# Sums of Strassen products formed in PSUM banks across products, in a hybrid encoder layer

## The chip, the cores and the metric

The kernel runs on one core of one Trainium2 chip. The core has a matrix engine (TensorE, PE in the views, with its weight loads as PEld), three engines for elementwise work (VectorE or DVE, ScalarE or ACT, GpSimd or POOL) and SyncE (SP), which here issues most DMA transfers. Each engine works through its own instructions in program order and waits on semaphores for the others. Matmuls write to PSUM, eight banks of 512 fp32 values on each of 128 partitions; everything else lives in SBUF. The metric is the device time of one execution in microseconds (us), as the median of several runs.

## The reference

One layer, fp32, 1024 tokens of width 1024:

```python
h = rmsnorm(x, norm_mix[l])
proj = h @ w_in[l]
q, k, v, r, lr_f, lr_b, u, g_a, g_b = jnp.split(proj, split_points, axis=-1)
...
o = o_fwd + o_bwd                              # gated linear attention, both directions
...
y_a = o @ w_branch_gla[l]
...
merged = jax.nn.sigmoid(g_a) * y_a + jax.nn.sigmoid(g_b) * y_b
x = x + merged @ w_out[l]
h2 = rmsnorm(x, norm_ffn[l])
gate, up = jnp.split(h2 @ w_ffn_in[l], 2, axis=-1)
x = x + (jax.nn.silu(gate) * up) @ w_ffn_out[l]
return rmsnorm(x, norm_final)
```

The hidden width of the feed-forward part (D_FF) is 2816, so w_ffn_in is 1024 x 5632. The change touches the last four products: w_branch_gla, w_out, w_ffn_in and w_ffn_out.

## The kernel before

**Three matmuls for one.** For fp32 accuracy each operand is split in a high and a low part (split_to, L172 and L173: a ScalarE cast makes the high part, named dh, gh, wh or oh, and VectorE or GpSimd subtracts it to get the low part, dl, gl, wl or ol). A product is then high x high, high x low and low x high, three matmuls (products, at L250) added up in one PSUM bank, with a contraction of 128 each.

**Strassen's seven products.** Each of the four large matrix products is cut in 2 x 2 quarters and done as the seven products of the Strassen-Winograd form, numbered P1 to P7, in place of eight. The four result quarters are

```
C00 = P1 + P2        C01 = P1 + P6 + P5 + P3
C10 = P1 + P6 + P7 + P4        C11 = P1 + P6 + P7 + P5
```

Operand sums go in ahead (VectorE and GpSimd); sums of products are formed after. Before, each product is added up in its own PSUM bank or banks, taken in turn from a cycle over all eight (mm_banks, three banks of the pool ps_mm, then five of ps_g). The collector reads it from there, and VectorE and GpSimd add the products in SBUF.

**The stages.** From 0 to about 575 us run the input projection, attention and pooling, which the change leaves alone. Then:

- Branch projection (BRANCH, o @ w_branch_gla) and merged projection (MERGED, merged @ w_out), by the function project: 48 matmuls a product, in four banks (m = 0..3) with c = 0 and 1 for the two halves of the contraction. After c = 1 each m is collected. collect_branch adds the products up in u2 and v2, and merge (L1041 to L1043) multiplies by the gate and adds the pooled branch, the latter on GpSimd. collect_out adds to the rows x2 of the residual, squares them for the norm (squares, L1224) and normalises them (xn).
- FFN-in: the normalised rows are transposed (L1176, L1179) and their quarter sums formed (features, L1194 to L1214), with their splits gh and gl, which stay for the whole stage. The weights come in 22 units of 128 gate channels and the 128 up channels that belong to them; one unit's seven products have 12 matmuls each in one bank. Gated.run collects them. The first three units run interleaved, product by product, while the features are still being made (units 0 and 1 through all seven products, unit 2 through P1 and P2); units 2 to 21 then run one by one, with the weight sums (combined, L1101, tile fs) and splits of coming products some four steps ahead (AHEAD). After each odd unit put_out (L1361 to L1364) forms the four operand sums for FFN-out on VectorE and sends seven pieces to DRAM; OutSums forms the weight sums for FFN-out on GpSimd (L1380 to L1386).
- FFN-out: 132 matmuls a product in four banks, the contraction in pieces that come back from DRAM (gor, wor) and are split into oh and ol. collect (L1549 and plus, L1510) adds each product into the residual rows x2; whole, second_half and first_half normalise and store the result.

**What sets the order.** The program's order is written out by hand: tuples of product numbers (BRANCH, MERGED, ORDER for FFN-in, OUT_ORDER) and explicit steps between them. Each engine keeps that order, so an instruction whose input is late holds up all that stand behind it on its engine.

## Time and profile before

| | |
|---|---|
| median of 3 runs | 1451.91 us (1451.48 to 1453.66) |
| profiled execution | 1452.8 us, of which the span of the trace is 1451.1 us |
| mean granted TensorE clock | 0.995 |
| instructions in the trace | 18652, of them 6797 matmuls |
| HBM read / written | 158.22 MB / 74.71 MB |

The views give times from the span's start, in us. A row of a timeline has start, duration, engine, line, operation and tiles (out<-in); in brackets stands how long the engine had been idle before it, and what it was released by. A row with x2 or more joins instructions that follow one another. A row of the chain has start, duration and the work that set the end there. The idle time of an engine that others don't wait for costs nothing.

### The profile page before, as it was taken

To read this page: it belongs to the slowest core of one execution; us is meant where nothing else is said; L and a number is where in the kernel's file an instruction comes from. 1 tells how busy PE (TensorE), PEld (TensorE's weight loads), DVE (VectorE), ACT (ScalarE), POOL (GpSimd) and SP (SyncE) were. 2 spreads that over 40 slices of the span, in tenths; PEclk is the share of its full clock that TensorE was granted. 3 is DMA by queue.
4 is the path that set the end of the run, shared out by engine and by line. 5 is a ranking of instruction groups with operands and counts; after the bars stand their busy time and mean duration, and the time that the engine had idled before them with its cause. 6 is when DMAs were issued, how large, how long until landed. Compare 5 with 4: busy or idle time off the path is not lost. (4 is left out here: it accounts for less than half of the span.)

```text
span 1451.1 us, 18652 instructions
## 1 busy us (share of the span) xinstructions
PE 1405.5 (97%) x6797; PEld 1179.6 (81%) x6797; DVE 872.5 (60%) x1111; ACT 561.8 (39%) x995; POOL 743.8 (51%) x510
## 2 busy tenths in 40 slices
PE   7999999999999999999999989999999999999988
PEld 6889898888888787888777778888888888778876
DVE  6266767662132463477994777777677777465375
ACT  6364655652122333344125523322323323444243
POOL 3240413222264553456743457666666668597355
PEclk9999999999999999999999999999999999999999
DMA  6120201011176768686666556444544446966362
GB/s 186 44 58 2 59 16 44 15 30 37 50 224 206 274 214 293 236 290 252 191 203 225 182 178 195 152 154 160 163 153 152 151 154 222 351 234 255 131 240 79
DMA packets 164732, 234.15 MB, mean 161 GB/s; under 512 B 10873, under 2 KB 97953, under 8 KB 164641
## 3 DMA queue, kind: packets, MB, share of 16 engines
q1 hardware_dynamic: 151936, 194.17, 40.7%
q10 hardware_dynamic: 12704, 38.80, 7.1%
q8 instruction: 53, 0.87, 0.2%
q14 instruction: 39, 0.31, 0.1%
HBM read 158.22 MB, written 74.71 MB: 161 GB/s over the span
## 5 line engine op out<-in xcount | busy, mean ns | idle before, releaser
L173 POOL TENSOR_TENSOR wl<-raw,wh 128x512 fp32r<-128x512 f32 (+1 forms) x91 | 124.6, 1387 | 257.3 <-ACT wh L172 212.4
L250 PE MATMUL ps<-gh,wl 128*128 128x512 f32 x616 | 240.8, 391 | 4.0 <-POOL wl L173 4.0
L250 PE MATMUL ps<-gh,wh 128*128 128x512 f32 x616 | 240.9, 391 | 0.1
L250 PE MATMUL ps<-gl,wh 128*128 128x512 f32 x616 | 240.2, 390 | 0.0
L250 PE MATMUL ps<-hh,wh 128*128 128x512 f32 x576 | 229.3, 398 | 5.2 <-ACT wh L172 5.2
L250 PE MATMUL ps<-hh,wl 128*128 128x512 f32 x576 | 226.1, 393 | 1.2 <-POOL wl L173 1.2
L250 PE MATMUL ps<-hl,wh 128*128 128x512 f32 x576 | 225.4, 391 | 0.0
L173 POOL TENSOR_TENSOR wl<-fs,wh 128x512 fp32r<-128x512 f32 x80 | 112.4, 1405 | 97.9 <-ACT wh L172 69.7
L250 PEld LDWEIGHTS ps<-gh,wl 128*128 128x128 f32 x616 | 116.0, 188 | 29.2 <-POOL wl L173 4.8
L172 ACT CAST wh<-fs 128x512 fp32r<-128x512 f32 x80 | 49.8, 622 | 230.2 <-DVE fs L1101 221.4
L250 PEld LDWEIGHTS ps<-gh,wh 128*128 128x128 f32 x616 | 116.1, 189 | 24.3 <-issue 0.5
L250 PEld LDWEIGHTS ps<-gl,wh 128*128 128x128 f32 x616 | 115.9, 188 | 23.8
L173 POOL TENSOR_TENSOR ol<-gor,oh 128x1024 fp32r<-128x1024 f32 (+1 forms) x42 | 109.2, 2617 | 47.0 <-ACT oh L172 46.1
L250 PEld LDWEIGHTS ps<-hh,wh 128*128 128x128 f32 x576 | 108.9, 189 | 27.0 <-ACT wh L172 6.0
L250 PEld LDWEIGHTS ps<-hh,wl 128*128 128x128 f32 x576 | 108.9, 189 | 25.3 <-POOL wl L173 2.1
L250 PEld LDWEIGHTS ps<-hl,wh 128*128 128x128 f32 x576 | 109.1, 189 | 21.3
L250 PE MATMUL ps<-oh,ol 128*128 128x512 f32 x308 | 120.2, 390 | 4.9 <-POOL ol L173 4.9
L250 PE MATMUL ps<-ol,oh 128*128 128x512 f32 x308 | 120.0, 389 | 2.9 <-DVE ol L173 2.9
L250 PE MATMUL ps<-oh,oh 128*128 128x512 f32 x308 | 120.0, 390 | 0.0
L173 DVE TENSOR_TENSOR ol<-wor,oh 128x1024 fp32r<-128x1024 f32 (+1 forms) x42 | 87.6, 2112 | 39.0 <-ACT oh L172 30.2
L173 POOL TENSOR_TENSOR wl<-fraw,wh 128x512 fp32r<-128x512 f32 x60 | 94.3, 1571 | 16.3 <-ACT wh L172 16.3
L250 PE MATMUL ps<-wh,hh 128*128 128x256 f32 x256 | 79.7, 311 | 0.0
(255 smaller groups left out, 2878.3 us busy)
## 6 DMA issues: line engine op xcount, KB each, us to landing
raw<-in_w_in_dram SPq DMA_DIRECT2D x88, 256.0 KB, 3.1
fraw<-in_w_ffn_in_dram SPq DMA_DIRECT2D x44, 512.0 KB, 5.6
gor<-g_out SPq DMA_DIRECT2D x35, 512.0 KB, 5.4
g_out<-s SPq DMA_DIRECT2D x44, 256.0 KB, 2.4
wor<-t_out SPq DMA_DIRECT2D x20, 512.0 KB, 8.2
g_out<-g SPq DMA_DIRECT2D x33, 256.0 KB, 3.4
x<-in_x_dram SPq DMA_DIRECT2D x16, 512.0 KB, 4.6
wor<-in_w_ffn_out_dram SPq DMA_DIRECT2D x15, 512.0 KB, 7.4
```

The source lines that it names most:

```text
L172: nc.scalar.copy(hi, src)
L173: eng.tensor_tensor(lo, src, as_f32(hi), op=ALU.subtract)
L250: nc.tensor.matmul(ps, a[i], b[j], start=first and n == 0, stop=last and n == 2)
```

## The change

Products that share their sums now go on in the same PSUM banks. P1, P6, P7 and P4 form one group: only P1 starts its bank afresh, and each later one is added on top (start is false), so that the bank holds P1, then P1 + P6, then P1 + P6 + P7, then C10 without more. P5 and P3 form a second group; P2 takes banks of the second kind by itself. A group of four-bank products uses U_BANKS (three of ps_mm, one of ps_g) or X_BANKS (four of ps_g), and a unit of FFN-in has one bank of ps_mm and one of ps_g. The collector reads the partial sum between two products of a group: by a ScalarE copy for P1, P6 and P5 in the branch projection and FFN-in, by VectorE additions elsewhere. In the merged projection the groups are P1, P6, P7, P2, P3 (with P2 and P3 starting afresh) on U_BANKS, and P4 and P5 on X_BANKS.

The product orders change with it:

| | before | after |
|---|---|---|
| BRANCH | 1 2 6 5 3 7 4 | 1 2 6 5 7 3 4 |
| MERGED | 1 7 6 5 4 2 3 | 1 4 6 7 5 2 3 |
| ORDER (FFN-in) | 1 6 2 7 4 5 3 | 1 2 6 5 7 3 4 |
| OUT_ORDER (FFN-out) | 1 6 2 5 3 7 4 | 1 2 6 5 3 7 4 |

The buffers p1s and u3 for sums in SBUF go. The diff, cut to its core (the tuples of the orders, the loads that follow them and the buffers for sums are left out):

```diff
     mm_banks = cycle([ps_mm])
-    def products(ps, a, b, first=True, last=True):
+    def products(ps, a, b, first=True, last=True, onto=False):
         for n, (i, j) in enumerate(((0, 0), (0, 1), (1, 0))):
-            nc.tensor.matmul(ps, a[i], b[j], start=first and n == 0, stop=last and n == 2)
-    def mm3(ps, a, b, first, last):
-        products(ps, a, b, first, last)
+            nc.tensor.matmul(ps, a[i], b[j], start=first and n == 0, stop=last and n == 2, skip_group_check=onto)
+    def mm3(ps, a, b, first, last, onto=False):
+        products(ps, a, b, first, last, onto)
         pump(ps.shape[-1] / HALF)
...
+    UP = (1, 6, 7, 4)
+    FIRST = (1, 2, 5)
     add = partial(nc.vector.tensor_tensor, op=ALU.add)
...
                 return merged[i, j][c][:, :, :]
-            if p == 7:
+            if p == 6:
                 s3s.append(slot(s="s3"))
                 sub(s3s[c][:, :, :], block(0, 0), block(1, 0))
-            elif p == 6:
                 padd(block(1, 0), block(1, 0), block(1, 1))
...
     mm_banks = cycle([ps_mm] * MM_BANKS + [ps_g] * (8 - MM_BANKS))
-    def project(base, products, collect, before, amid=None):
+    U_BANKS = [ps_mm] * 3 + [ps_g]
+    X_BANKS = [ps_g] * 4
+    def project(base, products, collect, before, amid=None, first=FIRST, up=UP, pools_of=lambda p: U_BANKS if p == 1 else X_BANKS):
+        banks = {}
         for at, p in enumerate(products):
             before(p)
-            sums = [bank(next(mm_banks)) for _ in range(4)]
+            if p in first:
+                banks[p in up] = [bank(pool) for pool in pools_of(p)]
+            sums = banks[p in up]
             for c in range(2):
...
                             sums[m][:, :], tuple(t[:, m * P : (m + 1) * P] for t in a[k]), b[k],
-                            c == 0 and k == 0, c == 1 and k == 1,
+                            c == 0 and k == 0 and p in first, c == 1 and k == 1, p not in first,
                         )
...
         sa, yb = (quarter(t, m) for t in gates[i, j])
-        add(dst, ps, s)
-        nc.vector.tensor_tensor(dst, dst, sa, op=ALU.mult)
+        if s is not None:
+            add(dst, ps, s)
+            ps = dst
+        nc.vector.tensor_tensor(dst, ps, sa, op=ALU.mult)
         padd(dst, dst, yb)
...
         u, v = quarter(u2, m), quarter(v2, m)
-        if p == 1:
-            nc.scalar.copy(u, ps)
-        elif p == 2:
-            merge(0, 0, m, ps, u)
-        elif p == 6:
-            add(u, ps, u)
-        elif p == 5:
-            add(v, ps, u)
-        elif p == 3:
-            merge(0, 1, m, ps, v)
-        elif p == 7:
-            merge(1, 1, m, ps, v)
-            add(u, ps, u)
+        if p in (1, 6, 5):
+            nc.scalar.copy(v if p == 5 else u, ps)
         else:
-            merge(1, 0, m, ps, u)
+            i, j = {2: (0, 0), 7: (1, 1), 3: (0, 1), 4: (1, 0)}[p]
+            merge(i, j, m, ps, {2: u, 7: v, 3: u}.get(p))
...
     def collect_out(p, m, ps):
-        p1, w = quarter(p1s, m), quarter(u3, m)
-        def x_of(i, j):
-            return x2[4 * (1 - i) + m][:, COLS[j]]
-        if p == 1:
-            nc.scalar.copy(p1, ps)
-            add(x_of(0, 0), x_of(0, 0), p1)
-        elif p == 7:
-            add(w, ps, p1)
-        elif p == 6:
-            add(w, ps, w)
-            add(p1, ps, p1)
-            padd(x_of(1, 1), x_of(1, 1), w)
-        elif p == 5:
-            for i in (1, 0):
-                add(x_of(i, 1), ps, x_of(i, 1))
-            add(x_of(1, 0), x_of(1, 0), w)
-            padd(x_of(0, 1), x_of(0, 1), p1)
-        else:
-            i, j = {4: (1, 0), 2: (0, 0), 3: (0, 1)}[p]
-            add(x_of(i, j), ps, x_of(i, j))
+        for i, j in {1: ((0, 0),), 6: ((0, 1),), 7: ((1, 0), (1, 1)), 5: ((0, 1), (1, 1)), 4: ((1, 0),), 2: ((0, 0),), 3: ((0, 1),)}[p]:
+            xs = x2[4 * (1 - i) + m][:, COLS[j]]
+            add(xs, ps, xs)
+        if p in (5, 2, 3):
             t = 4 * (1 - i) + m
...
                 xn[t] = slot(shape=(D,), s="xn")
-            for col in {4: (0, 1), 2: (0,), 3: (1,)}[p]:
+            for col in {5: (0, 1), 2: (0,), 3: (1,)}[p]:
                 squares(t, mss[t], xn[t], col)
...
             units[0].step(2)
-    project(len(BRANCH) * 2, MERGED, collect_out, before_out, amid_out)
+    project(
+        len(BRANCH) * 2, MERGED, collect_out, before_out, amid_out, (1, 2, 3, 4, 5), (1, 2, 3, 6, 7),
+        lambda p: X_BANKS if p in (4, 5) else U_BANKS
+    )
     normed()
     flush()
-    def product(unit, p, ps):
+    def product(unit, p, ps, right):
         for k in range(4):
             mm3(
-                ps[:, :], unit(p, k), tuple(t[:, k % 2, :] for t in split_b[p][k // 2]),
-                k == 0, k == 3,
+                ps[:, :], unit(p, k), tuple(t[:, k % 2, :] for t in right[p][k // 2]),
+                k == 0 and p in FIRST, k == 3, p not in FIRST,
             )
...
         def __init__(self, unit, in_slot=False):
-            self.unit, self.banks = unit, {}
+            self.unit, self.done = unit, set()
             self.g = slot(s="g") if in_slot else None
...
                 sums = slot(s="sums")
-                self.p16, self.p167 = sums[:, 0, :], sums[:, 1, :]
+                self.gate, self.up = sums[:, 0, :], sums[:, 1, :]
             elif not in_slot:
...
         def two_sums(self):
-            self.p16, self.p167 = t2(s="p16")[:, :], t2(s="p167")[:, :]
+            self.gate, self.up = t2(s="gate")[:, :], t2(s="up")[:, :]
         def run(self, p):
-            self.banks[p] = bank(next(mm_banks))
-            product(self.unit, p, self.banks[p])
-            ps = self.banks[p][:, :]
+            if p == 1:
+                self.u = bank(ps_mm)
+            elif p in FIRST:
+                self.x = bank(ps_g)
+            ps = self.u if p in UP else self.x
+            product(self.unit, p, ps, split_b)
+            self.done.add(p)
+            ps = ps[:, :]
             mul = partial(nc.vector.tensor_tensor, op=ALU.mult)
-            if p > 2:
-                p16, p167 = self.p16, self.p167
             if p == 1:
-                self.p1 = self.g[:, 0, :] if self.g else t2(s="p1")[:, :]
-                nc.scalar.copy(self.p1, ps)
+                self.sg = self.g[:, 0, :] if self.g else t2(s="sg")[:, :]
+                nc.scalar.copy(self.sg, ps)
             elif p == 2:
-                self.sg = self.p1 if 6 in self.banks else self.g[:, 1, :]
-                add(self.sg, ps, self.p1)
+                add(self.sg, ps, self.sg)
                 nc.scalar.activation(self.sg, self.sg, AF.Silu)
             elif p == 6:
-                add(p16, ps, self.p1)
+                nc.scalar.copy(self.gate, ps)
+            elif p == 5:
+                nc.scalar.copy(self.up, ps)
             elif p == 7:
-                add(p167, ps, p16)
-            elif p == 4:
+                add(self.up, ps, self.up)
+            elif p == 3:
+                add(self.gate, ps, self.gate)
+                nc.scalar.activation(self.gate, self.gate, AF.Silu)
+            else:
                 self.g = self.g or slot(s="g")
-                add(self.g[:, 0, :], ps, p167)
-                mul(self.g[:, 0, :], self.g[:, 0, :], self.sg)
-            elif p == 3:
-                add(p16, ps, p16)
-                nc.scalar.activation(p16, p16, AF.Silu)
-                mul(self.g[:, 1, :], p16, p167)
-            if p in (4, 5) and {4, 5} <= self.banks.keys():
-                self.fifth()
-        def fifth(self):
-            for s in (self.p167, self.p16):
-                nc.vector.tensor_tensor(s, self.banks[5][:, :], s, op=ALU.add)
+                mul(self.g[:, 0, :], ps, self.sg)
+            if p in (3, 7) and {3, 7} <= self.done:
+                self.g = self.g or slot(s="g")
+                mul(self.g[:, 1, :], self.gate, self.up)
     def put_out(q, ga, gb):
...
     def collect(p, m, ps):
-        p1 = p1s[m // 2][:, m % 2, :]
-        if p == 1:
-            nc.scalar.copy(p1, ps)
-            plus(nc.gpsimd, 0, 0, m, p1)
-        elif p == 6:
-            nc.vector.tensor_tensor(p1, ps, p1, op=ALU.add)
-            plus(nc.vector, 0, 1, m, p1)
-            for j in (1, 0):
-                plus(nc.gpsimd, 1, j, m, p1)
-        else:
-            for half, j in {2: ((0, 0),), 5: ((0, 1), (1, 1)), 3: ((0, 1),), 7: ((1, 1), (1, 0)), 4: ((1, 0),)}[p]:
-                plus(nc.vector, half, j, m, ps)
+        half, j = {1: (0, 0), 2: (0, 0), 6: (0, 1), 5: (1, 1), 7: (1, 1), 3: (0, 1), 4: (1, 0)}[p]
+        xs = x2[4 * half + m][:, COLS[j]]
+        add(xs, ps, xs)
         if p == 3:
...
+    banks = {}
     for at, p in enumerate(OUT_ORDER):
         closing = at == len(OUT_ORDER) - 1
-        sums = [bank(next(mm_banks)) for _ in range(4)]
+        if p in FIRST:
+            banks[p in UP] = [bank(pool) for pool in (U_BANKS if p == 1 else X_BANKS)]
+        sums = banks[p in UP]
         for i in range(CLOSE if closing else n_of):
```

How instructions move, at three places. A name with a number is one tile; the numbers of the two kernels differ.

On ScalarE, at the start of FFN-in, before: the silu of P2 (L1337) and the casts of the features (gh), then those of weights (wh).

```order
L1337 ACTIVATE g_7196<-g_7196 128x512
L172 CAST gh_7405<-hb_6995 128x1024
L172 CAST gh_7407<-hb_6996 128x1024
L172 CAST gh_7428<-hb_7242 128x1024
L172 CAST gh_7430<-hb_7243 128x1024
L172 CAST wh_7522<-fs_7520 128x512
```

And now, with copies of P5 (L1328) and of P6 (L1326) of units 0 and 1:

```order
L1324 ACTIVATE g_7144<-g_7144 128x512
L172 CAST gh_7353<-hb_6943 128x1024
L172 CAST gh_7355<-hb_6944 128x1024
L1328 COPY sums_7141<-ps_7346 128x512
L172 CAST gh_7377<-hb_7190 128x1024
L172 CAST gh_7379<-hb_7191 128x1024
L1328 COPY sums_7143<-ps_7370 128x512
L1326 COPY sums_7141<-ps_7149 128x512
L1326 COPY sums_7143<-ps_7167 128x512
L172 CAST wh_7468<-fs_7466 128x512
```

The copies came in behind the casts; the matmuls of P7 write to the banks that the L1326 copies read.

On VectorE, at the border between an odd and an even unit of the FFN-in loop, before: P3's and P5's additions, put_out's sums, then the next unit.

```order
L1355 TENSOR_TENSOR p_1555_8058<-ps_8168,p_1555_8058 128x512
L1101 TENSOR_TENSOR fs_8187<-fraw_7964,fraw_7966 128x512
L1347 TENSOR_TENSOR p_1555_8058<-ps_8193,p_1555_8058 128x512
L1349 TENSOR_TENSOR g_8161<-p_1555_8058,p_1556_8059 128x512
L1361 TENSOR_TENSOR s_1588_8209<-g_8009,g_8161 128x512
L1362 TENSOR_TENSOR s_1588_8209<-s_1588_8209,g_8009 128x512
L1363 TENSOR_TENSOR s_1589_8210<-g_8009 128x512
L1364 TENSOR_TENSOR s_1589_8210<-g_8161,s_1588_8209 128x512
L1339 TENSOR_TENSOR p_1590_8222<-ps_8247,p_1595_8241 128x512
L1101 TENSOR_TENSOR fs_8262<-fraw_7964,fs_8142 128x512
```

And now:

```order
L1332 TENSOR_TENSOR gate_7974<-ps_8043,gate_7974 128x512
L1339 TENSOR_TENSOR g_8096<-gate_7974,up_7975 128x512
L1336 TENSOR_TENSOR g_8096<-ps_7982,sg_7995 128x512
L1345 TENSOR_TENSOR s_1535_8119<-g_7951,g_8096 128x512
L1346 TENSOR_TENSOR s_1535_8119<-s_1535_8119,g_7951 128x512
L1347 TENSOR_TENSOR s_1536_8120<-g_7951 128x512
L1348 TENSOR_TENSOR s_1536_8120<-g_8096,s_1535_8119 128x512
L1103 TENSOR_TENSOR fs_8134<-fraw_7887,fraw_7889 128x512
L1103 TENSOR_TENSOR fs_8155<-fraw_7887,fs_8076 128x512
```

The sums now follow P4's multiplication (L1336), and both weight sums (fs) of coming products stand behind them, where one stood ahead.

On VectorE, at the border of the branch and the merged projection, before: the fourth tile of P7, the two splits for the first merged product, its operand sum (L918), and P4's first tile.

```order
L1041 TENSOR_TENSOR mg_6313<-ps_6254,sum_5769 128x512
L1042 TENSOR_TENSOR mg_6313<-mg_6313,gate_6050 128x512
L1059 TENSOR_TENSOR sum_5767<-ps_6254,sum_5767 128x512
L173 TENSOR_TENSOR dl_6369<-mg_5924,dh_6368 128x1024
L173 TENSOR_TENSOR dl_6405<-mg_5925,dh_6404 128x1024
L918 TENSOR_TENSOR s_1210_6408<-mg_5924,mg_6211 128x1024
L1041 TENSOR_TENSOR mg_6416<-ps_6356,sum_5766 128x512
L1042 TENSOR_TENSOR mg_6416<-mg_6416,gate_6140 128x512
```

And now, with P3 in the place of P7:

```order
L1052 TENSOR_TENSOR mg_6301<-ps_6055,sum_5767 128x512
L1054 TENSOR_TENSOR mg_6301<-mg_6301,gate_6046 128x512
L173 TENSOR_TENSOR dl_6349<-mg_5924,dh_6348 128x1024
L173 TENSOR_TENSOR dl_6385<-mg_5925,dh_6384 128x1024
L1054 TENSOR_TENSOR mg_6394<-ps_5778,gate_6136 128x512
L1054 TENSOR_TENSOR mg_6394<-ps_5779,gate_6136 128x512
```

The third operation of each tile has gone, the operand sum stands later, and P4 has one operation a tile.

More of the change, by code (lines that the diff above doesn't have):

```diff
@@ L852, in data_split @@
         return [(hi[:, k, :], lo[:, k, :]) for k in range(2)]
-    BRANCH = (1, 2, 6, 5, 3, 7, 4)
+    BRANCH = (1, 2, 6, 5, 7, 3, 4)
     WEIGHT_A = {1: (0, 0), 2: (0, 1), 4: (1, 1)}
@@ L891 @@
     line += [branch_piece(p, c) for p in BRANCH for c in range(2)]
-    MERGED = (1, 7, 6, 5, 4, 2, 3)
+    MERGED = (1, 4, 6, 7, 5, 2, 3)
     merged = {}
@@ L1046, in collect_branch @@
         u, v = quarter(u2, m), quarter(v2, m)
-        if p == 1:
-            nc.scalar.copy(u, ps)
-        elif p == 2:
-            merge(0, 0, m, ps, u)
-        elif p == 6:
-            add(u, ps, u)
-        elif p == 5:
-            add(v, ps, u)
-        elif p == 3:
-            merge(0, 1, m, ps, v)
-        elif p == 7:
-            merge(1, 1, m, ps, v)
-            add(u, ps, u)
-        else:
-            merge(1, 0, m, ps, u)
+        if p in (1, 6, 5):
+            nc.scalar.copy(v if p == 5 else u, ps)
+        else:
+            i, j = {2: (0, 0), 7: (1, 1), 3: (0, 1), 4: (1, 0)}[p]
+            merge(i, j, m, ps, {2: u, 7: v, 3: u}.get(p))
     x2 = [None] * NT
     def before_branch(p):
-        if p in (1, 6, 5, 3):
-            load_gates(*{1: (0, 0), 6: (0, 1), 5: (1, 1), 3: (1, 0)}[p])
-        if p in (7, 4):
-            for t in range(4 * (p == 7), 4 * (p == 7) + 4):
+        if p in (1, 6, 5, 7):
+            load_gates(*{1: (0, 0), 6: (1, 1), 5: (0, 1), 7: (1, 0)}[p])
+        if p in (3, 4):
+            for t in range(4 * (p == 3), 4 * (p == 3) + 4):
                 x2[t] = slot(shape=(D,), s="x2")
@@ L1073 @@
     project(0, BRANCH, collect_branch, before_branch)
-    ORDER = (1, 6, 2, 7, 4, 5, 3)
+    ORDER = (1, 2, 6, 5, 7, 3, 4)
     xn = [None] * NT
@@ L1232, in two_scale @@
         return rs
-    p1s, u3 = ([slot(s="sum") for _ in range(2)] for _ in range(2))
     mss = {}
@@ L1333, in run @@
             elif p == 2:
-                self.sg = self.p1 if 6 in self.banks else self.g[:, 1, :]
-                add(self.sg, ps, self.p1)
+                add(self.sg, ps, self.sg)
                 nc.scalar.activation(self.sg, self.sg, AF.Silu)
             elif p == 6:
-                add(p16, ps, self.p1)
+                nc.scalar.copy(self.gate, ps)
+            elif p == 5:
+                nc.scalar.copy(self.up, ps)
             elif p == 7:
-                add(p167, ps, p16)
-            elif p == 4:
-                self.g = self.g or slot(s="g")
-                add(self.g[:, 0, :], ps, p167)
-                mul(self.g[:, 0, :], self.g[:, 0, :], self.sg)
-            elif p == 3:
-                add(p16, ps, p16)
-                nc.scalar.activation(p16, p16, AF.Silu)
-                mul(self.g[:, 1, :], p16, p167)
@@ L1389, in sums @@
                 nc.sync.dma_start(t_out[p][:, self.q, :], src)
-    OUT_ORDER = (1, 6, 2, 5, 3, 7, 4)
+    OUT_ORDER = (1, 2, 6, 5, 3, 7, 4)
     PIECES = [(q, min(2, PAIRS - q)) for q in range(0, PAIRS, 2)]
@@ L1494 @@
     x2 = []
-    p1s = [slot(s="p1s") for _ in range(2)]
     gain_final = slot(shape=(D,), s="gfin")
@@ L1506 @@
     scales = {}
-    def plus(eng, half, j, m, src):
-        xs = x2[4 * half + m][:, COLS[j]]
-        eng.tensor_tensor(xs, xs, src, op=ALU.add)
     def whole(t):
@@ L1561, in collect, with piece_product @@
             first_half(4 + m)
-    def piece_product(ps, n, m, first, last):
+    def piece_product(ps, n, m, first, last, onto):
         w, g = ready_pieces[n]
@@ L1568, in piece_product @@
                 ps[:, :], tuple(t[:, q, m * P : (m + 1) * P] for t in g), tuple(t[:, q, :] for t in w),
-                first and q == 0, last and q == c - 1,
+                first and q == 0, last and q == c - 1, onto,
             )
@@ L1585 @@
             for m in range(4):
-                piece_product(sums[m], n, m, i == 0, i == n_of - 1)
+                piece_product(sums[m], n, m, i == 0 and p in FIRST, i == n_of - 1, p not in FIRST)
                 if i == n_of - 1:
@@ L1597 @@
                 for i in range(CLOSE, n_of):
-                    piece_product(sums[m], at * n_of + i, m, False, i == n_of - 1)
+                    piece_product(sums[m], at * n_of + i, m, False, i == n_of - 1, p not in FIRST)
                 collect(p, m, sums[m][:, :])
```

## The prediction

> **What bounds the kernel now.** I read the page's busy times first, then the busy time by stretch, then the chain that ended last, and then the timeline of each engine around the places where TensorE stood idle.

> The page's busy times:

> ```profile
> PE 1405.5 (97%) x6797; PEld 1179.6 (81%) x6797; DVE 872.5 (60%) x1111; ACT 561.8 (39%) x995; POOL 743.8 (51%) x510
> ```

> The busy time of the FFN-in loop, of TensorE, its weight loads, VectorE, ScalarE and GpSimd in this order:

> ```profile
> 862.00:1223.00 361.00, 360.65 (x1585) 298.49 (x1586) 254.29 (x279) 108.58 (x188) 258.45 (x177) 1.00 0.50 166
> ```

> The reader should see that TensorE is the bound, and that in the FFN-in loop it idles 0.35 us of 361. The change keeps all 6797 matmuls. Vector additions that vanish there are therefore worth nothing by themselves: VectorE is busy 254 of those 361 us and has room anyway. Time can only be won from the idle of TensorE outside the loop, and lost wherever a new wait stops it. The chain says the same, one unbroken piece of matmuls:

> ```profile
> 862.35 360.35 PE ps L250 x1582
> ```

> This gives the scale: 360.35 / 1582 = 0.228 us a matmul, 2.73 us for a 12-matmul product of a FFN-in unit, 10.9 us for a 48-matmul product of the projections.

> The idle pieces that the change can touch, from TensorE's timeline, each with what released it:

> ```profile
> 711.70 0.50 PE L250 MATMUL ps<-wh,dl 128*128 128x512 f32 x1 [1.54 <-DVE dl L173]
> 734.64 0.50 PE L250 MATMUL ps<-wh,dl 128*128 128x512 f32 x1 [0.84 <-DVE dl L173]
> ...
> 862.35 0.80 PE L250 MATMUL ps<-gh,wl 128*128 128x512 f32 x1 [3.79 <-POOL wl L173]
> ...
> 865.50 0.40 PE L250 MATMUL ps<-gh,wh 128*128 128x512 f32 x1
> ...
> 1249.50 0.50 PE L250 MATMUL ps<-oh,ol 128*128 128x512 f32 x1 [1.70 <-POOL ol L173]
> ...
> 1306.24 0.50 PE L250 MATMUL ps<-oh,ol 128*128 128x512 f32 x1 [2.01 <-POOL ol L173]
> ...
> 1399.05 0.50 PE L250 MATMUL ps<-ol,oh 128*128 128x512 f32 x1 [2.94 <-DVE ol L173]
> ```

> Together 12.8 us, and the 3.79 us idle costs more than itself: eight starts from 862.35 to 865.50 take 3.15 us where seven steps of 0.228 would take 1.59, so about 1.6 us go to matmuls at half rate (0.80 us the first shown, 0.40 the last).

> **What the change adds.** A product that goes on in a bank may not begin before the collector has read the previous product from it. Before, a product took the next bank in a rotation over eight. Now P6 waits for the copy of P1, P7 for the copy of P6, P4 for the addition of P7, and P3 for the copy of P5. Mostly one whole product lies between, and the copy is short:

> ```profile
> 866.41 0.59 ACT L1332 COPY p<-ps 128x512 f32<-128x512 f32 x1 [4.69 <-PE ps L250]
> ```

> With 2.73 us or more of slack for 0.59 us this costs nothing, unless the copy stands behind something late on its in-order engine. [...] I looked for late readers at each stage.

> **Branch to merged projection, about +1.3 us.** The first merged product reuses the bank group in which the branch's P4 has just ended, so it needs P4's first multiplication, which VectorE runs after two subtractions for the split (dl). VectorE before:

> ```profile
> 700.61 0.68 DVE L1041 TENSOR_TENSOR mg<-ps,sum 128x512 f32<-128x512 f32 x1
> ...
> 709.12 0.68 DVE L1059 TENSOR_TENSOR sum<-ps,sum 128x512 f32<-128x512 f32 x1
> 709.73 3.05 DVE L173 TENSOR_TENSOR dl<-mg,dh 128x1024 fp32r<-128x1024 f32 x2
> ```

> Four tiles of three operations took 9.1 us up to 709.73. Without the third operation (4 x 0.6) they could end at 707.3 to 709.7, the later end if GpSimd's additions hold the multiplications up as here. Then two dl (3.05), then the multiplication (0.68): 711.1 to 713.5, where TensorE started at 711.70 before. I take 713.0, nearer the late end, since the same GpSimd additions remain: +1.3, bounds 0 and +1.8.

> **Merged projection, about -0.1 us.** The third product's operand sums no longer come late, so the 0.84 at 734.64 goes. But each tile of the fifth product now takes two additions from PSUM ahead of its norm in place of one, 0.6 us more a tile by the spacing above; only the last tile's share can reach TensorE, since it works on while the others come. I place that at 0.7. Bounds -0.84 and +1.

> **Start of FFN-in, about +3.5 us.** Three units run interleaved, and unit 0's P7 must wait for the copy of its P6. On ScalarE this copy now stands behind the last casts of the features and two copies of P5. The same casts before, and the GpSimd work that makes VectorE late ahead of them:

> ```profile
> 825.84 1.05 ACT L172 CAST gh<-hb 128x1024 fp32r<-128x1024 f32 x1 [1.72 <-DVE hb L1214]
> 830.33 2.95 ACT L172 CAST gh<-hb 128x1024 fp32r<-128x1024 f32 x3 [3.44 <-DVE hb L1214]
> ```

> ```profile
> 815.53 12.54 POOL L173 TENSOR_TENSOR gl<-hb,gh 128x1024 fp32r<-128x1024 f32 x4 [12.60 <-ACT gh L172]
> ```

> ```profile
> 725.41 2.04 ACT L1253 COPY sum<-ps 128x512 f32<-128x512 f32 x4
> ```

> Nothing ahead of 830.33 gets earlier: VectorE's same order of feature subtractions releases it. So the copy of P6 ends at 830.33 + 2.95 for three casts + 3 x 0.51 = 834.8. Counting products of 12 matmuls from TensorE's timeline, P7 would start with this row:

> ```profile
> 827.50 0.39 PE L250 MATMUL ps<-gh,wl 128*128 128x512 f32 x1
> ```

> That is an idle of 7.3 us. It will cost half-rate matmuls too (1.6 by the rows above). What pays some back is the 3.79 us idle at 862.35, which waits for FFN-out weights that in turn wait for the first outputs. Between 827.5 and 862.35 TensorE has 34.85 - 3.79 = 31.1 us of work, so unit 3 starts at 834.8 + 31.1 + 1.6 = 867.5 at full rate, against 862.35 + 1.6 lost behind it: +3.5. The outputs come some 5 us later, so those weights land about then as well. Bounds: if the copies were not late, -3.8 - 1.6 at best; if the weights wait longer than TensorE, +7.3.

> **FFN-in loop, about +1.4 us.** After nine pairs of units VectorE forms four sums for FFN-out (put_out). These now stand directly ahead of the weight sum whose cast stands on ScalarE ahead of the next unit's copy of P1, and P6 waits for that copy. Undisturbed sums and those in the loop:

> ```profile
> 850.20 0.69 DVE L1361 TENSOR_TENSOR s<-g,g 128x512 f32<-128x512 f32 x1
> ...
> 852.74 0.68 DVE L1101 TENSOR_TENSOR fs<-fraw,fs 128x512 f32<-128x512 f32 x1
> ...
> 922.92 1.67 DVE L1361 TENSOR_TENSOR s<-g,g 128x512 f32<-128x512 f32 x1
> ...
> 928.64 0.68 DVE L1339 TENSOR_TENSOR p<-ps,p 128x512 f32<-128x512 f32 x1
> ```

> From the eviction of P4: multiplication 0.72, sums 2.54, weight sum 0.68, cast 0.63 with its start, copy 0.59 = 5.2 us, against two products, 5.46, less some 0.2 to 0.3 until P4's eviction starts. That is no stall to 0.4 each. With the loop's slow sums (5.72) it is 3.2 us more, nine times 3.2 = 29 us. They were slow because GpSimd was running a weight subtraction:

> ```profile
> 924.71 1.75 POOL L173 TENSOR_TENSOR wl<-fs,wh 128x512 fp32r<-128x512 f32 x1 [0.66 <-ACT wh L172]
> ```

> In the new order the next weight sum, and with it GpSimd's next subtraction, stands behind the sums, so GpSimd has run dry by the second of them. I take the undisturbed row and 0.15 each: +1.4, bounds 0 and 29.

> **End of FFN-in and FFN-out, about -3.3 us.** The last product is now P4 with one multiplication, not P3 with an addition, an activation and a multiplication. VectorE before:

> ```profile
> 1226.98 0.68 DVE L1347 TENSOR_TENSOR p<-ps,p 128x512 f32<-128x512 f32 x1
> 1228.36 0.69 DVE L1349 TENSOR_TENSOR g<-p,p 128x512 f32<-128x512 f32 x1 [0.70 <-ACT p L1348]
> ```

> The last multiplication could run at 1226.98 in place of 1228.36: the last outputs come 1.4 us sooner, off the 1.70 at 1249.50. I take -1.3, bounds 0 and -1.7. GpSimd's twelve additions into x vanish, and with them the 2.01 idle at 1306.24, which these held up:

> ```profile
> 1298.67 5.22 POOL L1510 TENSOR_TENSOR x<-x,p1s 128x512 f32<-128x512 f32 x3
> ```

> -2.0, bounds 0 and -2.0. P3 follows P5 in its banks, and P4 follows P7, but with three tiles between one tile's end and its next start; I put no cost on it. The 2.94 at 1399 hangs on the final norm and stays.

> **Clock.** A new idle near 2.8 us at the start of the merged projection could bring half-rate matmuls. The rows differ: 2.94 us at 1399.05 is followed by a matmul of 0.50 like every short idle, while these two pauses, 3.4 us in all, were followed by matmuls of 0.61:

> ```profile
> 498.69 0.50 PE L250 MATMUL ps<-hh,wh 128*128 128x512 f32 x1 [2.75 <-ACT wh L172]
> ...
> 500.04 0.61 PE L250 MATMUL ps<-hh,wl 128*128 128x512 f32 x1 [0.62 <-POOL wl L173]
> ```

> I leave it out of the sum; with it the sum would be 1.6 higher. [...]

> **Sum.** 1.3 - 0.1 + 3.5 + 1.4 - 3.3 = +2.8 on the profiled execution, 1452.8 around a span of 1451.1 us (1.7 us outside it, unchanged). That execution is 0.9 above the median of the runs, 1451.91, so the forecast is about 1454.7. A measurement here can tell about 0.2%, 2.9 us, from no change: faster is below 1449.0, slower above 1454.8.

> **Rivals.**
> 1. *The new waits are hidden* (0.27). The copies at the start of FFN-in run before P7 needs them and everything else pays: -0.8, -1.3, -2.0 and 2 to 4 of the idle at 862.35, some -7: 1445. For it: ScalarE idles 3.44 us just ahead of 830.33, and another order of release would let copies through. Against it: the engine works in order, and the cast that it waits for stands ahead of the copies.
> 2. *The sums in the loop stay slow* (0.14). Nine stalls of about 3 us, a sum of +2.8 - 1.4 + 29: about 1482; with half of it, 1468. For it: all the loop's sums before are stretched. Against it: the row at 850.20 with GpSimd idle. It decides as soon as the sums take more than 2.9 us.
> 3. *FFN-out stalls on its consecutive products* (0.07). P3's first matmul waits for a late addition of P5, since VectorE also splits the operands there, 1.5 us for each (3.05 for two, above). Two or three of these ahead of each of two product borders, 6 to 9 us over the forecast if nothing lies between: about 1462. Against it: about 4 us (18 matmuls) lie between.

> **How the numbers follow.** The forecast's own case holds 0.52, with a range of 1449 to 1460 from the bounds of its terms. The range for 8 in 10 takes in rival 1 to 1445 and rival 2 with half its stalls: 1445 to 1468. Faster: rival 1 and a little of the forecast, 0.29. Within 0.2%: not quite half of the forecast's case, 0.24. Slower: the other half, rivals 2 and 3, 0.47.

> **What would show it.** In the timeline of TensorE: an idle of about 7 us near 828, released by a ScalarE copy of L1326, then matmuls at half rate; little or no idle near 867; 2 to 3.5 us at 713; none at 735 and 1306. In the loop: the copies of L1321 ending within 5.5 us of P4's multiplication, and put_out's sums taking 2.5 us. I am wrong if the copies at 828 run ahead of the casts, if TensorE shows nine idles of 2 us or more in the loop, or if the weights of unit 3 keep it waiting beyond 868.

## The result, and the profile after

The changed kernel took 1459.33 us (median of 6 runs, 1457.99 to 1462.07) against 1452.33 (6 runs) for the kernel before: slower, ratio 1.005, interval 1.0037 to 1.0063. The forecast was 1454.7, slower was the likeliest case at 0.47, and the range ended at 1468. So direction and mechanism came out as forecast, and the size was 7.0 us where 2.8 had been summed up. The sum alone stood just under the prediction's own line for slower (1454.8); what made the result clear is in good part half clock, which the sum left out.

The page's busy times after the change:

```profile
PE 1408.5 (97%) x6797; PEld 1183.0 (81%) x6797; DVE 724.2 (50%) x995; ACT 583.8 (40%) x1039; POOL 682.1 (47%) x490
```

VectorE is busy 148 us less than before and GpSimd 62 us less, and the span grew from 1451.1 to 1457.8. TensorE was the bound, so the relief bought nothing where TensorE was busy. What changed is where TensorE idles. Its timeline, with the idle ahead of each row and what ended it:

```profile
712.88 0.76 PE L251 MATMUL ps<-wh,dh 128*128 128x512 f32 x1 [2.92 <-issue]
713.44 0.63 PE L251 MATMUL ps<-wl,dh 128*128 128x512 f32 x1
...
804.89 0.33 PE L1178 MATMUL tr<-ident,xn 128*128 128x128 f32 x1 [1.27 <-DVE xn L287]
...
837.91 0.80 PE L251 MATMUL ps<-gh,wh 128*128 128x512 f32 x1 [7.54 <-ACT sums L1326]
...
871.69 0.50 PE L251 MATMUL ps<-gh,wl 128*128 128x512 f32 x1 [1.36 <-POOL wl L173]
...
1257.89 0.50 PE L251 MATMUL ps<-oh,ol 128*128 128x512 f32 x1 [1.42 <-POOL ol L173]
...
1405.09 0.79 PE L251 MATMUL ps<-ol,oh 128*128 128x512 f32 x1 [2.95 <-DVE ol L173]
...
1423.33 0.50 PE L251 MATMUL ps<-oh,oh 128*128 128x512 f32 x1 [0.38 <-DVE x L1525]
```

The reader should see four things. The forecast wait of 7.3 us for a ScalarE copy of P6 is there, 7.54 us. The wait at the border of branch and merged projection is 2.92 us, and the matmuls behind it take 0.63, not 0.39. The idle at 1405 is as long as before (2.94), but this time a matmul of 0.79 follows it. The last row is small but of a new kind: in FFN-out P4 waits for an addition (L1525) that reads P7 from the same bank. The releaser "issue" at 712.88 is a blank in the profile; VectorE's row says what it was. First the two splits, then P4's four multiplications, of which the first ends at about 712.8:

```profile
707.66 4.51 DVE L173 TENSOR_TENSOR dl<-mg,dh 128x1024 fp32r<-128x1024 f32 x2
712.10 2.47 DVE L1054 TENSOR_TENSOR mg<-ps,gate 128x512 f32<-128x512 f32 x4
```

ScalarE at the start of FFN-in, where the late copies stand:

```profile
833.46 1.04 ACT L172 CAST gh<-hb 128x1024 fp32r<-128x1024 f32 x1 [3.40 <-DVE hb L1216]
834.41 0.58 ACT L1328 COPY sums<-ps 128x512 f32<-128x512 f32 x1
834.89 1.99 ACT L172 CAST gh<-hb 128x1024 fp32r<-128x1024 f32 x2
836.78 0.59 ACT L1328 COPY sums<-ps 128x512 f32<-128x512 f32 x1
837.26 1.08 ACT L1326 COPY sums<-ps 128x512 f32<-128x512 f32 x2
```

This is the queue that the prediction built, row for row, 3.1 us later because the work ahead was late by that much. ScalarE had idled 3.40 us ahead of it, from 830.06; TensorE had ended P6 by 830.4, so the copies were ready in that time and could not pass the cast that waited.

The table splits up by how much the changed kernel lies behind the kernel before at successive places, from the rows of both timelines. The forecast column has the terms of the prediction:

| stretch | measured us | forecast us |
|---|---|---|
| wait at branch to merged projection (711.70 to 712.88) | +1.2 | +1.3 |
| half clock behind it (14 steps take 6.0, at full rate 3.2) | +2.8 | 0 |
| merged projection and norm | -0.8 | -0.1 |
| start of FFN-in, to the end of the first product of unit 3 | +4.7 | +3.5 |
| FFN-in loop | +1.0 | +1.4 |
| end of FFN-in, up to 1257.89 | -0.5 | -1.3 |
| FFN-out up to 1405.09 | -2.4 | -2.0 |
| half clock behind 1405.09 (+1.5) and smaller idles to the end (-0.8) | +0.7 | 0 |
| sum | +6.7 | +2.8 |

In the loop the four sums of put_out took no more than the undisturbed time, as argued, one pair as an example:

```profile
929.97 0.68 DVE L1345 TENSOR_TENSOR s<-g,g 128x512 f32<-128x512 f32 x1
930.69 0.69 DVE L1346 TENSOR_TENSOR s<-s,g 128x512 f32<-128x512 f32 x1
...
933.11 0.68 DVE L1103 TENSOR_TENSOR fs<-fraw,fs 128x512 f32<-128x512 f32 x1
```

### The profile page after: what moved, and what is told of

It reads as the page before. It is cut to its first block, busy times and chain, and to the rows that moved or that the text cites. A ratio compares the mean times of both kernels' runs of the same rounds, so it can differ in the third digit from the quotient of the medians.

```text
span 1457.8 us, 18429 instructions
## 1 busy us (share of the span) xinstructions
PE 1408.5 (97%) x6797; PEld 1183.0 (81%) x6797; DVE 724.2 (50%) x995; ACT 583.8 (40%) x1039; POOL 682.1 (47%) x490
## 5 line engine op out<-in xcount | busy, mean ns | idle before, releaser
L173 POOL TENSOR_TENSOR wl<-raw,wh 128x512 fp32r<-128x512 f32 (+1 forms) x91 | 124.5, 1386 | 257.3 <-ACT wh L172 212.5
L173 POOL TENSOR_TENSOR wl<-fs,wh 128x512 fp32r<-128x512 f32 x80 | 106.2, 1344 | 102.8 <-ACT wh L172 102.8
L173 POOL TENSOR_TENSOR ol<-gor,oh 128x1024 fp32r<-128x1024 f32 (+1 forms) x42 | 102.4, 2447 | 73.2 <-ACT oh L172 69.9
L172 ACT CAST wh<-fs 128x512 fp32r<-128x512 f32 x80 | 49.3, 617 | 165.8 <-DVE fs L1103 153.0
L173 DVE TENSOR_TENSOR ol<-wor,oh 128x1024 fp32r<-128x1024 f32 (+1 forms) x42 | 71.6, 1726 | 51.4 <-ACT oh L172 38.4
L173 POOL TENSOR_TENSOR wl<-fraw,wh 128x512 fp32r<-128x512 f32 x60 | 78.2, 1304 | 36.4 <-ACT wh L172 35.1
L1330 DVE TENSOR_TENSOR up<-ps,up 128x512 f32<-128x512 f32 x20 | 13.8, 691 | 137.1 <-PE ps L251 137.1
```

Source lines behind the costliest of these rows:

```text
L172: nc.scalar.copy(hi, src)
L173: eng.tensor_tensor(lo, src, as_f32(hi), op=ALU.subtract)
L1330: add(self.up, ps, self.up)
```

## The experiments

The theory to test: the loss sits in two new waits, and in the half clock that they bring. Its rivals: the norm's chain or the late features would hold TensorE up at the same places anyway.

**Other banks for the merged projection (e1_other_banks).** Its first product no longer uses the banks that P4 has just filled.

```diff
-        lambda p: X_BANKS if p in (4, 5) else U_BANKS
+        lambda p: U_BANKS if p in (4, 5) else X_BANKS
```

> The changed kernel with one edit: in the merged projection the two bank groups are swapped, so that its first product goes into the banks from which the branch's P3 was read, and no longer waits for P4's first multiplication. Theory (the wait of 2.92 us at 712.88 and the 6.83 us of half clock behind it cost 1.4 us more wait and 2.95 us of rate than before): the first matmul is released by the first dl near 710, the idle there is under 1.5 us, no half clock follows, the profiled span falls by 4 to 5 us from 1457.8, time about 1455. Rival (a later wait takes it back, since the norm's chain behind the merged projection sets the start of FFN-in): the idle at 712 goes but a new one stands at 777 or 805, and the time falls by less than 2 us.

Measured: 1455.31 us (11 runs), against 1452.67 for the kernel before; ratio 1.002 (1.0012 to 1.0029). That is 4.0 us under the changed kernel. In TensorE's timeline the border has no idle at all, not even the 1.54 us of the kernel before, and the rows keep the full rate:

```profile
708.79 0.39 PE L251 MATMUL ps<-dh,wl 128*128 128x512 f32 x1
709.01 0.39 PE L251 MATMUL ps<-wh,dh 128*128 128x512 f32 x1
```

A part came back later: 2.20 us of idle end at 774.79, which the changed kernel does not have, and in this execution 3.41 us at half clock follow them (775.95 to 779.36). So the rival has a share: against the changed kernel's timeline 6.0 us are won at the border, and 3.3 of them are left behind the transposes. The theory carries the verdict.

**The gap filled with useless matmuls (e2_filled_gap).** The wait stays, only TensorE does not stand still in it. If the half clock comes from the idle itself, it goes with the gap.

```diff
-            if p in first:
+            if p in first and not (base and p == 4):
...
                 a, b = made[n]
+                if base and at == 0 and c == 0:
+                    banks[False] = [bank(pool) for pool in X_BANKS]
+                    for _ in range(11):
+                        nc.tensor.matmul(banks[False][0][:, :], a[0][0][:, :P], b[0][0], start=True, stop=True)
```

> The changed kernel with 11 matmuls added whose result is thrown away (2.5 us at full rate), in the gap ahead of the merged projection's first product, on that product's own operands and into a bank that the fourth product starts afresh later. The wait for P4's multiplication stays as it is. [...] Rival (the slow matmuls come with the first use of these banks or of weights from DRAM): the 0.63 us matmuls stay and the time falls by less than 0.5 us or rises.

Measured: 1456.57 us (7 runs), 2.8 under the changed kernel; 1456.5 had been forecast. TensorE's timeline, the eleven added matmuls in the first row:

```profile
707.63 2.65 PE L1023 MATMUL ps<-wh,dh 128*128 128x512 f32 x11
710.70 0.50 PE L251 MATMUL ps<-wh,dh 128*128 128x512 f32 x1 [0.41 <-DVE mg L1058]
711.04 0.40 PE L251 MATMUL ps<-wl,dh 128*128 128x512 f32 x1
```

The same matmuls on the same banks run at full rate, and the releaser is now named: P4's multiplication (mg). The first product starts at 710.70 and not near 712.9 because this execution was 2.2 us ahead all the way to the border; the wait is the same. So the half clock belongs to the idle and not to the banks or the weights. In the trace of the changed kernel it costs 2.8 us, and the medians differ by as much. The execution of e9 below bears this out from another side: there the gap is not filled (2.93 us), and no half clock followed, with the same banks and weights. Together e1 and e2 split the border's loss: 2.8 for the clock, 1.2 for the wait.

**P7 apart in the first two units (e3_p7_apart).** There P7 starts a bank of its own and P4 goes on in that one; the copy of P1 + P6 is added on VectorE.

```diff
-    def product(unit, p, ps, right):
+    def product(unit, p, ps, right, first=FIRST):
...
-                k == 0 and p in FIRST, k == 3, p not in FIRST,
+                k == 0 and p in first, k == 3, p not in first,
...
             ps = self.u if p in UP else self.x
-            product(self.unit, p, ps, split_b)
+            apart = self.unit in units[:2]
+            if apart and p == 7:
+                self.y = bank(ps_g)
+            if apart and p in (7, 4):
+                ps = self.y
+            product(self.unit, p, ps, split_b, FIRST + (7,) if apart else FIRST)
...
                 add(self.up, ps, self.up)
+                if apart:
+                    add(self.up, self.up, self.gate)
...
+                if apart:
+                    add(self.g[:, 1, :], ps, self.gate)
+                    ps = self.g[:, 1, :]
                 mul(self.g[:, 0, :], ps, self.sg)
```

> The changed kernel with one edit: for the first two FFN-in units alone, P7 starts a bank of its own and P4 goes on in that one; the copy of P1 + P6 is added on VectorE, as before the change. P7 then does not wait for the copies at 837. Theory (that wait of 7.54 us and its 1.9 us of half clock is what the start of FFN-in loses; behind it the old wait for the first FFN-out weights comes back, 3 to 4 us with 1.6 of half clock): no idle over 1.5 us between 815 and 850, an idle of 3 to 4 us near 865, the span falls by 4 to 6 us, time about 1454. Rival (the features themselves are late, whichever bank is used, so P7 or P4 waits for a cast or a subtraction instead): an idle of 4 us or more stays near 835 with another releaser, the time falls by less than 2 us.

Measured: 1454.92 us (11 runs), 4.4 under the changed kernel. TensorE at the two places:

```profile
836.52 0.50 PE L251 MATMUL ps<-gh,wh 128*128 128x512 f32 x1 [0.64 <-DVE sums L1335]
```

```profile
866.00 0.80 PE L251 MATMUL ps<-gh,wl 128*128 128x512 f32 x1 [3.72 <-POOL wl L173]
```

The wait of 7.54 us has become 0.64, and the old wait for the FFN-out weights, hidden under it, is back with 3.72 us and its half clock. The features were in time; the copies were the cause.

**Both edits (e4_both).**

> Both edits, other banks in the merged projection and P7 apart in the first two units. Theory: the two gains add up, 8 to 11 us off 1459.3, about 1449.5, below the kernel before (1452.3), since what is left of the change are its gains at the end (the idle at 1306 gone). Rival (the two share one bound, the norm's chain or the first FFN-out weights): about the better of the two single edits, 1453 to 1455.

Measured: 1451.29 us (11 runs), 8.0 under the changed kernel where the single edits gave 4.0 and 4.4. The gains add up. Against the kernel before the ratio is 0.999 (0.998 to 1.0): with its two waits out, the change is worth about 1.4 us, with an interval that just reaches nothing, and not the 3 that had been expected.

**The change in FFN-out alone (e5_out_only).** The kernel before, with the part of the diff that concerns OUT_ORDER, collect, piece_product and the banks of that loop.

> The kernel before with the change made in FFN-out alone (P1, P6, P7, P4 and P5, P3 going on in their banks there, product order unchanged but for P2 and P6; all stages ahead as before). Theory: the idle of 2.01 us at 1306 and most of the 1.20 us at 1406 go, no idle stands at the borders P5 to P3 and P7 to P4; the idle of 2.9 us behind P3's norm stays but begins 2 us earlier, at 1394.1. [...] Rival (the consecutive products stall): idles of 1 to 4 us near 1365 and 1430, time not below 1452.

Measured: 1450.92 us (11 runs) against 1452.49; ratio 0.9987 (0.9978 to 0.9996); 1451 to 1452 had been forecast. No idle stands at the border of P5 and P3, and that at 1306 is gone; at the border of P7 and P4 P4's third tile waits 0.39 us for an addition of P7 (at 1417.29). The idle behind P3's norm, 2.96 us up to 1398.89, turned expensive. The stretch in which it ends and the next one, with TensorE's busy time first behind the length and, third from the end, the granted clock:

```profile
1396.95:1400.37 3.42, 1.48 (x6) 1.24 (x7) 1.89 (x1) 0.00 (x0) 0.81 (x1) 1.00 1.00 308
1400.37:1403.78 3.41, 3.41 (x9) 2.65 (x8) 1.23 (x1) 2.46 (x3) 0.29 (x1) 0.50 1.03 401
```

Half clock follows for 3.41 us. In this execution part of what FFN-out saves is given back there; it is the slowest of the eleven (1453.48), so how often that happens no trace shows.

**Weights early (e6_both_weights_early and e7_before_weights_early).** What is left is the idle of 3.7 to 3.9 us at about 861, which the kernel before has too. The version with both edits (e6) and the kernel before (e7) each get this one edit:

```diff
-    put_out(0, *(y.g for y in first[:2]))
     g_pair, out_sums, summing = [], [OutSums(0)], None
+    put_out(0, *(y.g for y in first[:2]))
```

> Both edits of before (other banks in the merged projection, P7 apart in the first two units), and the load of the first FFN-out weights (OutSums(0)) stands ahead of put_out on the DMA queue. Theory: the idle of 3.87 us at 861 waits for these weights alone, so it goes with its half clock (1.6 to 1.9 us); the span falls by 5 to 6 us against the two edits (1451.3), time about 1446. Rival (GpSimd's weight subtraction is late for another reason, its split behind the weight sums): an idle of 2 us or more stays near 860, time above 1449.

> The kernel before with the load of the first FFN-out weights alone moved ahead of put_out. It tells whether the version with all edits wins by the change or by this move. Theory: the idle of 3.79 us at 862 and its 1.6 us of half clock go, time about 1447, so that what the change is worth, once its new waits are out, is about 1 to 2 us. Rival (the change itself is worth more, since VectorE is freer): this kernel stays at 1450 or above and the version with all edits is 3 us or more faster.

Measured: 1446.39 us (5 runs) with both edits, ratio 0.9959 (0.9946 to 0.9971); 1449.83 us (11 runs) on the kernel before, ratio 0.9984 (0.9975 to 0.9993). On the kernel before the edit brought 2.7 us where 5 had been expected, though the idle at 862 has shrunk to this:

```profile
857.34 0.50 PE L250 MATMUL ps<-gh,wl 128*128 128x512 f32 x1 [0.37 <-POOL wl L173]
```

With the same edit on both sides the change with its waits out is 3.4 us faster than without, more than the 1 to 2 expected. The interval of e4 reaches up to 2.9 us, and this difference has, by an estimate from its two intervals, some 2 us either way, so it does not contradict the 1.4 of e4. The two traces show where most of it comes from: the idles of 1.54 and 0.86 us in the merged projection and of 2.01 us in FFN-out are gone, and at 775 stand 2.20 in place of 0.67. So the change has a value, but only once its waits are out.

**Sums ahead of a split (e8_sums_before_split).** On top of e6, at the end of FFN-in:

```diff
-    early = {1: "l", 2: "l", 3: "s", 4: "l", 5: "s", 6: "ls"}
+    early = {1: "l", 2: "l", 3: "s", 4: "l", 5: "s", 6: "l"}
...
             put_out(n // 2, *g_pair)
+            if n == FT - 1:
+                split_piece()
```

> The version with all edits (1446.4), and at the end of FFN-in the last pair's put_out stands ahead of one operand split for FFN-out (an ol subtraction on VectorE and one on GpSimd) that stood in front of it. Theory (this split is why the idle at the start of FFN-out stayed, 1.42 us after the change against 1.70 before, where 0.4 had been forecast): the sums start 2.5 us sooner, the idle of 1.3 us at 1244 goes to under 0.5, time lower by 1 us. Rival (the split is itself on the path, or the DMA queue's order sets it): the idle stays or moves to the next pieces, time the same or higher.

Measured: 1444.85 us (6 runs), ratio 0.9939 (0.9926 to 0.9952): the fastest version of the study, 8.8 us under the kernel before in the same comparison (1453.6). TensorE shows no idle over 0.15 us at the start of FFN-out. The step over e6 is 1.5 us, with intervals that overlap a little.

**Longer sums in the loop (e9_longer_sums).** The changed kernel, with one of put_out's sums written three times:

```diff
-        nc.vector.tensor_tensor(s34[:, 0, :], a11, a21, op=ALU.subtract)
+        for _ in range(3):
+            nc.vector.tensor_tensor(s34[:, 0, :], a11, a21, op=ALU.subtract)
```

> The changed kernel with two more VectorE subtractions in every put_out (they repeat one of its four, 0.6 us each, same result). It measures the slack of the new wait at the nine borders of the FFN-in loop, where the trace shows 0.2 us between the end of the copy of P1 and the start of P6. [...] Rival (the wait has a whole product of slack, 2.7 us): no idle in the loop, the time stays at 1459.3.

Measured: 1475.53 us (5 runs, 1470.02 to 1476.04). TensorE, the first two of nine such rows:

```profile
894.17 0.50 PE L251 MATMUL ps<-gh,wh 128*128 128x512 f32 x1 [1.14 <-ACT sg L1321]
...
933.68 0.50 PE L251 MATMUL ps<-gh,wh 128*128 128x512 f32 x1 [1.14 <-ACT sg L1321]
```

VectorE's three equal subtractions, and the matmul that stands ahead of the first of these rows:

```profile
889.57 2.13 DVE L1348 TENSOR_TENSOR s<-g 128x512 f32<-128x512 f32 x3
891.62 0.68 DVE L1349 TENSOR_TENSOR s<-g,s 128x512 f32<-128x512 f32 x1
```

```profile
892.64 0.39 PE L251 MATMUL ps<-gh,wl 128*128 128x512 f32 x1
```

From the start of the three to the next sum 2.05 us pass where one took 0.60, so 1.45 are added. P6 starts 1.53 us behind the matmul ahead of it where 0.23 is the full rate, so it is 1.30 late. The slack was about 0.15 us, close to the 0.2 read from the trace. The rows lie 39.51 us apart, where two units of 84 matmuls take 38.1: 1.4 a border, 12.6 for nine, where 9 had been forecast (two subtractions of 0.6 less a margin of 0.2, nine times). The rest of the 16 us was not forecast. Two runs took 1470.0 us at a mean granted clock of 0.992, three 1475.5 to 1476.0 at 0.988 to 0.989, and a clock lower by 0.0035 over 1470 us is 5 us; in which places these three lost it, no trace shows.

## Why the prediction was right, and where its sizes were off

*TensorE is the bound, fewer additions buy nothing in the loop.* Right. In the loop's 361 us VectorE (the third busy time) works 154.8 us where it worked 254.3, and the loop grew by 1.0:

```profile
871.00:1232.00 361.00, 359.93 (x1585) 297.29 (x1586) 154.82 (x204) 126.58 (x225) 233.32 (x177) 1.00 0.51 166
```

*Start of FFN-in, copy of P6 behind casts.* Right in place, cause and length (7.3 forecast, 7.54 measured); e3 shows it. The sum of the stretch was too small, 3.5 against 4.7. The missing step: the FFN-out weights were put down as landing "about then as well". They did land then, but GpSimd takes their first subtraction ahead of the weight split (wl) that unit 3 needs, so 1.36 us of idle followed at 871.69:

```profile
868.69 1.73 POOL L1364 TENSOR_TENSOR wot<-wot 128x512 f32<-128x512 f32 x1 [9.14 <-DMA wot<-in_w_ffn_out_dram]
870.38 1.25 POOL L173 TENSOR_TENSOR wl<-fraw,wh 128x512 fp32r<-128x512 f32 x1
```

One of the prediction's own signs of being wrong, that the weights of unit 3 keep it waiting beyond 868, has so come true in small.

*Branch to merged projection.* The wait was right, 1.3 forecast and 1.2 measured, with P4's first multiplication done at 712.8 where 713.0 had been taken. That the size fits so well is partly luck: the four tiles ahead were done at 707.7, near the early bound and not near the late one that was taken, and the two splits took 4.4 us where 3.05 had been read from the kernel before. The step that failed is the one under the heading Clock: half clock was left out of the sum, with a price of 1.6 beside it. It came, and cost 2.8 (e2), since it lasted 6.82 us. That a pause of under 3 us stays free of half clock, as the sum had it, no run shows: 2.94 us did in the kernel before, and 2.92 us in the changed kernel did not.

*Loop borders.* Right: no stall of note, +1.0 against +1.4, and the sums undisturbed (0.68 to 0.69 us each) with GpSimd idle for 4.12 us up to 934.00, where the row of 1.67 in the kernel before had it at work (1.30 us from 922.75). Rival 2 did not come about, but its point of decision was real: e9 shows a margin of about 0.15 us.

*Merged projection.* -0.8 against -0.1. The 0.84 went as forecast. Of the small idles ahead of the transposes 0.67 went and 0.25 grew to 1.27, together +0.35. That growth stands where the price of 0.7 for the second addition would show, but e1 keeps the two additions and has 0.23 there, so the price is not shown. Some 0.3 us of the -0.8 are traced to no row.

*End of FFN-in.* -1.3 was taken, -0.5 came, of which 0.28 in the idle itself. P4's one multiplication did spare the chain of P3, but another operand split (2.68 us on VectorE) got in ahead of the sums, and they began no sooner after the last product. e8, which moves that split behind them, has the idle gone; it was run on the version with the other edits, so for the changed kernel itself this is argued.

*FFN-out.* -2.4 against -2.0, and rival 3, long stalls at the consecutive products, did not come about (e5). But its wait is there in small. The prediction counted 18 matmuls between a tile's end and the next product's start on its bank; that holds for the last of the four tiles alone. The last piece of a product has 3 matmuls a tile and the first piece of the next 6, so it is 9, 12, 15 and 18. P4's third tile waited 0.38 us in the changed kernel, and 1.51 in e2. Not foreseen: the idle at 1405, unchanged in length, was followed by half clock this time, 1.5 us.

Rival 1, the new waits hidden, fell with the first row at 837.91.

## What to carry to other kernels

When products go on in one PSUM bank, list for each the reader of the bank before it, and look on that reader's engine at what stands ahead of it in program order: a ready copy of 0.6 us cost 7.5 us of TensorE because it stood behind a cast that waited. Give a product a bank of its own at the few places where its reader is late (first units, 4.4 us in e3; borders of stages, 4.0 us in e1), and keep the shared bank in the steady loop. Where TensorE is the bound, price a new idle twice, once as idle and once as the half clock that may follow it: behind the idles of 2.92, 2.95 and 7.54 us in the changed kernel it cost 2.8, 1.5 and 1.9 us.

## What the runs showed of the hardware

```profile
708.55:711.97 3.42, 1.41 (x7) 0.83 (x5) 3.42 (x2) 0.00 (x0) 2.54 (x2) 1.00 0.52 160
711.97:715.38 3.41, 2.50 (x6) 2.05 (x7) 3.41 (x6) 0.00 (x0) 2.53 (x3) 0.50 0.60 190
715.38:718.79 3.41, 3.41 (x9) 2.64 (x9) 3.41 (x3) 0.00 (x0) 3.41 (x2) 0.50 0.00 0
```

Matmuls of 128x512 start 0.43 us apart there (713.44 to 713.87), and 0.23 behind it (718.90 to 719.13).

Among pauses of about 2.2 and 2.9 us the length did not tell whether half clock followed. At the border of branch and merged projection 2.92 us had it behind them in the changed kernel. In e9 a pause of 2.93 us at the same place did not:

```profile
707.59:711.00 3.41, 1.48 (x7) 0.90 (x5) 3.41 (x2) 0.00 (x0) 2.62 (x2) 1.00 0.56 154
711.00:714.42 3.42, 2.43 (x11) 2.02 (x12) 3.42 (x6) 0.00 (x0) 2.45 (x2) 1.00 0.66 201
```

Behind P3's norm 2.95 us in the changed kernel and 2.96 us in e5 were followed by half clock, and 2.94 us in the kernel before were not:

```profile
1394.55:1397.97 3.42, 1.56 (x7) 0.94 (x6) 3.42 (x3) 0.72 (x1) 2.57 (x1) 1.00 0.43 149
1397.97:1401.38 3.41, 2.33 (x10) 1.95 (x11) 1.03 (x1) 0.51 (x1) 0.00 (x0) 1.00 0.97 317
```

The idle of 2.20 us that ends at about 775 had both outcomes too. In e1 the clock behind it was 0.50:

```profile
775.95:779.36 3.41, 3.41 (x11) 2.73 (x10) 1.35 (x3) 3.28 (x7) 0.79 (x1) 0.50 0.05 14
```

In e4 it stayed at 1.00:

```profile
776.75:780.17 3.42, 3.42 (x20) 2.85 (x19) 1.58 (x3) 3.39 (x8) 1.26 (x1) 1.00 0.24 81
```

What decides between the two is not shown: no run moves a pause and leaves all else as it is. The fastest runs of the changed kernel, 1457.99 us, have mean granted clocks of 0.991 and 0.992, the slowest, 1462.07 us, has 0.988; 0.003 of 1460 us is 4 us. So by an estimate from these numbers the clock is one reason why runs of one kernel spread by 2 to 6 us here.
